# h kept in DRAM as the two parts of its split, in place of the unsplit h

## The chip, the core and the metric

The kernel runs on one core of a Trainium2 chip. The metric is the device time of one execution, in microseconds (us); lower is better. Engines: PE is TensorE (its weight loads are listed as PEld), DVE is VectorE, ACT is ScalarE, POOL is GpSimd, SP is SyncE, which issues nearly all DMAs here. A name with a q (SPq) is that engine's sequencer, which issues DMAs and waits.

## The reference

One layer of a streaming encoder on a prompt of 4096 tokens and a sample of 64, with 1024 features. Cut to what matters here:

```python
h = rms_norm(x, g_pre) * (1 + scale) + shift          # (T, 1024), scale and shift from c
q_a, k_a, v_a, z_a, a_lr, q_h, f_h, i_h, z_h = split(h @ w_in)
o_a = chunked_gla(q_a, k_a, v_a, log_alpha(a_lr))      # GLA, 4 heads
f = lb + (1 - lb) * sigmoid(f_h)
o_h = chunked_gla(silu(q_h), 1 - f, i_h, log(f))       # HGRN2, 4 heads
o = concat(rms_norm(o_a) * silu(z_a), rms_norm(o_h) * silu(z_h)) @ w_out
y = x + gate * rms_norm(o, g_post)
```

Everything is float32. All projections read the same h. The outputs are y for prompt and sample and the final states of both recurrences.

## The kernel before

**Products in parts.** A float32 product is made of three float32r products: each operand is split into a high part (a copy to float32r on ACT, L93) and a low part (the source less the high part, on DVE, L94); `split` (L87) issues both. Then high times high, high times low and low times high are added up in PSUM.

**Stages.** Tokens go in 16 groups of 256; the 64 sample tokens ride along with one group (T = 320 in place of 256), the last one in phase 1 and group 2 afterwards. Features are eight blocks of 128 (KT = 8), features on partitions. There are four stages, and each runs over all groups before the next begins, since the weights of one stage fill the weight room:

1. Phase 1 (GLA). For each group: load x, normalise, transpose and modulate it to h (`x_turn`), split h, project it (`proj_gla`), run the recurrence (`attend_group`). The unsplit h is stored to DRAM, `h_d` (and `h_s` for the sample), for the two stages that need it again.
2. HGRN. h is loaded from `h_d` (`load_hf`), split again, projected (`proj_hgrn`), and the recurrence runs. Its result goes to DRAM, `oh_d`.
3. The gate part. h is loaded and split a third time; `z_tile` projects one tile of 128 tokens (24 matmuls of 512 columns) and multiplies silu(z) into the HGRN result, which it loads from `oh_d` and stores back (L1299, L1308). The split of w_out runs beside it.
4. The output projection (`project`), which does not use h.

**The rooms of h.** Pool `h` has two tags. `hf` has four tiles of two blocks each, unsplit (float32); together one group. `hh` has five tiles, each with both parts of two blocks, so one group takes four of the five. A phase 1 group fills the four `hf` in `x_turn`; an HGRN or gate group fills them by `load_hf`. Then `split_h` makes four `hh`. The fifth `hh` lets the first split of a group start while the group before is still being projected; each further one waits until a pair of blocks of that group has been used for the last time, in the last token tile's product (`proj_tok`, L625; feature-side products are `proj_feat`, L613).

**Order.** The kernel is written against a framework that orders the instructions: it keeps a list per engine, with the order of the code as priority and its own estimate of when operands and rooms are ready, and places all semaphores. Each engine, SP with its DMAs among them, then works through its list in order, so an instruction that waits holds those behind it. `weave` runs a main generator (the projections of a group) and side generators (the recurrence of the group before as `side`, preparation of the next group as `prep`, loads of weights) in turns; the tuple (generator, n, first, last) spreads n steps between two steps of the main one.

**Lines that matter below.** The stores of h in phase 1 are L574 and L576, that of group 0 is L1663, the loads L581 and L583, `split_h` L585. `pair_up` (L595) copies the sample's columns of h on POOL. x is loaded at L475 (groups 0 and 1) and L482, and squared for its norm at L491 and L510. L1215 is the last DVE step of a recurrence result in HGRN and L1216 its store; L711 to L967 are the DVE chain of the recurrence that ends in the operands of the PE products at L1017; L1305 to L1308 end a gate tile.

Of the kernel before, what the change touches and what calls it, by code (L numbers as in the profile page):

```python
# [6 lines left out]
F32 = mybir.dt.float32  # L7
F32R = mybir.dt.float32r
# [7 lines left out]
P = 128  # L16
D = 1024
KT = D // P
GROUP = 256
# [9 lines left out]
class Kernel:  # L29
# [107 lines left out]
    def setup(self):  # L137
        nc, t, ctx = self.nc, self.t, self.ctx
        c = self.pool(ctx, "const")
        self.small = self.pool(ctx, "small", 4)  # L140
        self.wpool = self.pool(ctx, "w")

        self.wstage = self.pool(ctx, "wstage", 2, side="right")
        self.halves = []
        self.ep = self.pool(ctx, "e", side="right")
        self.h_room = ctx.enter_context(ExitStack())
        self.hp = self.pool(self.h_room, "h", side="right")
        self.x_room = ctx.enter_context(ExitStack())
        self.xp = self.pool(self.x_room, "x", side="right")
        self.pp = self.pool(ctx, "psum", 1, PSUM)  # L150
        dram = self.pool(ctx, "scratch", 1, DRAM)
        self.h_d, self.oa_d, self.oh_d = [], [], []
        for g, tl in enumerate(self.groups):
            self.h_d.append(dram.tile([P, KT, GROUP], F32, name=f"h_d{g}"))
            self.oa_d.append([dram.tile([r, 512], F32, name=f"oa_d{g}_{j}") for j, (_, _, r, _) in enumerate(tl)])
            self.oh_d.append([dram.tile([r, 512], F32, name=f"oh_d{g}_{j}") for j, (_, _, r, _) in enumerate(tl)])
        self.h_s = dram.tile([P, KT, self.dec], F32, name="h_s")
        self.gate_d = dram.tile([2, D], F32, name="gate_d")
        self.gate_p = dram.tile([8, 512], F32, name="gate_p")

        nc.scalar.preload_act_table_set("natural_log_exp_and_others")
        self.ident = c.tile([P, P], F32, name="ident")
        self.col = col = c.tile([P, 52], F32, name="col")
        self.c4 = c.tile([P, KT, 4], F32R, name="c4")
        self.md = c.tile([P, 2, KT, 2], F32, name="md")
        self.sh, self.gs = self.md[:, 0], self.md[:, 1]
        self.mask = c.tile([P, NMASK], U8, name="mask")
        self.member = c.tile([P, 12], F32, name="member")
        self.half = c.tile([P, 2], F32, name="half")
        self.balpha = col[:, 40:42]  # L170
        self.lb = c.tile([P, 4], F32, name="lb")
        self.oml = c.tile([P, 4], F32, name="oml")
        self.wal = c.tile([80, 256], F32R, name="wal")
        self.ats = [c.tile([P, 80], F32R, name=f"at{i}") for i in range(3)]

        with ExitStack() as s:
            one = self.pool(s, "setup")
            ap = self.pool(s, "ada", 3)

            rows = one.tile([52, P], F32, name="rows")  # L180
            v = lambda a: a.rearrange("(k p) -> k p", p=P)
            self.x_load(0, [0])
            nc.sync.dma_start(rows[0:8], v(t["c_prompt"][0]))
            nc.sync.dma_start(rows[8:16], v(t["c_sample"][0]))
            nc.sync.dma_start(self.ident, t["ident"])
            self.x_load(0, [1])
            few = [
                (rows[16:32], v(t["b_ada"][0, : 2 * D])),
                (rows[32:40], v(t["g_pre"][0])),
                (rows[40:42], v(t["b_alpha"][0])),  # L190
                (rows[42:50], t["hgrn_lb_logits"].rearrange("r (k p) -> (r k) p", p=P)),
                (rows[50:51], t["g_onorm_gla"]),
                (rows[51:52], t["g_onorm_hgrn"]),
            ]
            ada = self.ada_load(ap, 0, few[:4])
            w = self.first_load(0)
            for dst, src in few[4:]:
                nc.sync.dma_start(dst, src)
            with self.tc.manual_schedule():
                self.first_group(ap, ada, w, rows)  # L200
            for _ in self.vs0:
                pass
# [17 lines left out]
    def first_group(self, ap, ada, w, rows):  # L220


        nc, col = self.nc, self.col
        W = self.W1
        T = GROUP
# [98 lines left out]
        pr = self.ps("ms")  # L324
        nc.tensor.transpose(pr[:, :52], rows, self.ident[:52, :52])
        ada_sum(pa, parts.pop(0), [(1, 0), (1, 1)])
        self.hf = [self.hp.tile([P, 2, T], F32, name="hf", bufs=4) for _ in range(4)]
        nc.vector.tensor_copy(col[:, 16:], pr[:, 16:52])
        nc.vector.tensor_scalar(col[:, 24:32], col[:, 24:32], 1.0, None, ALU.add)
        raw(0, nc.scalar)  # L330
# [153 lines left out]
    def x_norm(self, g, js):  # L484

        nc = self.nc
        ss = self.small.tile([P, 2], F32, name="x_ss")
        for i, j in enumerate(js):
            xt, r = self.xs[j], self.groups[g][j][2]
            junk = self.hp.tile([P, 2, GROUP], F32, name="hf", bufs=4).rearrange("p k c -> p (k c)")  # L490
            nc.scalar.activation(  # L491
                junk.bitcast(mybir.dt.bfloat16)[:r], xt[:r], AF.Square, accum_out=ss[:r, i : i + 1]
            )
        rs = self.rstd(ss[:r, : len(js)], D, table=True)
        for i, j in enumerate(js):
            nc.vector.tensor_scalar(self.xs[j][:r], self.xs[j][:r], rs[:, i : i + 1], None, ALU.mult)
# [30 lines left out]
    def x_turn(self, g):  # L527
# [1 line left out]
        nc = self.nc  # L529
        tl = self.groups[g]  # L530
        T = self.tokens(tl)
        self.hf = hf = [self.hp.tile([P, 2, T], F32, name="hf", bufs=4) for _ in range(4)]
        for tiles, cnd in (([0, 1], 0), ([2], 1)):
            if tiles[0] >= len(tl):
                continue
# [22 lines left out]
            for i in range(4):  # L558
# [11 lines left out]
                    else:  # L570
                        nc.vector.tensor_scalar(dst, dst, sc, bi, ALU.mult, ALU.add)
                yield
        for i in range(4):
            nc.sync.dma_start(self.h_d[g][:, 2 * i : 2 * i + 2, :], hf[i][:, :, :GROUP])  # L574
            if len(tl) == 3:
                nc.sync.dma_start(self.h_s[:, 2 * i : 2 * i + 2, :], hf[i][:, :, GROUP:])  # L576

    def load_hf(self, g, tl):
        self.hf = [self.hp.tile([P, 2, self.tokens(tl)], F32, name="hf", bufs=4) for _ in range(4)]
        for i in range(4):  # L580
            self.nc.sync.dma_start(self.hf[i][:, :, :GROUP], self.h_d[g][:, 2 * i : 2 * i + 2, :])  # L581
            if len(tl) == 3:
                self.nc.sync.dma_start(self.hf[i][:, :, GROUP:], self.h_s[:, 2 * i : 2 * i + 2, :])  # L583

    def split_h(self):  # L585

        out = []
        T = self.hf[0].shape[2]
        for i in range(4):
            u = self.hp.tile([P, 2, 2, T], F32R, name="hh", bufs=5)  # L590
            self.split(u[:, 0], u[:, 1], self.hf[i])
            out.append(u)
        return lambda k: out[k // 2][:, :, k % 2]

    def pair_up(self, h, rooms):  # L595

# [1050 lines left out]
    def run(self):  # L1647
# [11 lines left out]
        with ExitStack() as rec:  # L1659
            self.open_recurrence(rec)  # L1660
            self.setup_late()
            for i in range(4):
                nc.sync.dma_start(self.h_d[0][:, 2 * i : 2 * i + 2, :], self.hf[i])  # L1663
            h = lambda k: self.h0[k // 2][:, :, k % 2]
            S, Ss = [None], [t["state_gla"]]
            side = None
# [9 lines left out]
                yield from self.x_turn(g)  # L1676

            def prep_h(g, tl):
                self.load_hf(g, tl)
                yield  # L1680

            for g in range(ng):
                prep = prep_x(g + 1) if g + 1 < ng else prep_h(0, self.groups2[0])
                sides = [(side, 12, 1, 18), (prep, 8, 0, 16) if g == 0 else (prep, 10, 3, 19)]
                if g == ng - 1:

                    sides.append((self.weights(W2["f"], C_FH, 512, "wa"), 10, 8, 18))
                    sides.append((self.weights(W2["q"], C_QH, 512, "wv"), 10, 20, 26))
                res = self.weave(self.proj_gla(g, h), sides)
                h = self.split_h()  # L1690
                side = self.attend_group(g, S, Ss, res, 2, 2, self.oa_d, t["new_gla_p"], t["new_gla_s"])
                next(side)
            S, Ss = [None], [t["state_hgrn"]]
# [2 lines left out]
            for g in range(ng):  # L1696
# [7 lines left out]
                if g == ng - 1:  # L1704
                    sides.append((self.weights(W3["z"], C_ZH, 512, "wa"), 10, 8, 18))
                res = self.weave(self.proj_hgrn(g, h), sides)
                h = self.split_h()
                side = self.attend_group(g, S, Ss, res, 4, 1, self.oh_d, t["new_hgrn_p"], t["new_hgrn_s"])
                next(side)
            now(gate)  # L1710
# [3 lines left out]
            def zrun():  # L1714
                hh = h
                for i, (g, j, tl) in enumerate(tiles):
                    if j == 0 and i > 0:
                        hh = self.split_h()
                        if len(self.groups2[g]) == 3:
                            self.pair_up(hh, [self.stage_pair(F32R)])  # L1720
                    if j == 0 and g + 1 < ng:
                        self.load_hf(g + 1, self.groups2[g + 1])
                    yield from self.z_tile(hh, tiles[i])
                    self.done += 1
                    yield
# [75 lines left out]
```

## Time and profile before

| | before |
|---|---|
| median of 3 runs | 2094.87 us (2094.38 to 2095.93) |
| profiled execution, time / span | 2090.48 us / 2088.7 us |
| PE, DVE, ACT busy | 98%, 75%, 53% of the span |
| granted PE clock, mean | 0.997 |
| DMA: bytes, mean rate | 190.15 MB, 91 GB/s |
| 128 loads `hf<-h_d`, 64 stores `h_d<-hf` | 256 KB each |
| splits of h (L93 on ACT, L94 on DVE), 188 of each | 625 ns and 697 ns, mean |

How to read it: the median is over executions without the profiler's view; the profile shows one execution, so sums made from its rows are compared with its own time. A row of an instruction group gives line, engine, operation, output<-inputs, shapes and count; then busy time and the mean ns of one; then the engine's idle time just before and what ended it. A row of a stage gives its length and each engine's busy time, the granted PE clock as a share of full speed, the DMA engines' busy share and the rate. A row of the timeline or the chain begins with its start and its length in us; [..] holds the idle time before it and what ended that. A busy PE is not PE at its peak, as matmuls overlap.

### The profile page before, as it was taken

What the parts mean: (1) busy time and instruction counts of PE and PEld (TensorE: products, weight loads), DVE (VectorE), ACT (ScalarE), POOL (GpSimd) and SP (SyncE); (2) the same over time, 40 slices, a digit from 0 to 9 for tenths busy, and PEclk for the clock granted to TensorE, in tenths of its full rate; (3) what the DMA queues carried; (4) which work ended last, traced back from release to release, by engine and by line L of the source; (5) the groups of instructions that cost most, each with busy time, mean ns of one, the idle gap of its engine ahead of it and who ended that gap; (6) DMA issues with size and microseconds to landing.
All of it is one profiled execution on the core that took longest, in us unless ns stands there. A gap on an engine that the chain in (4) does not pass through costs nothing.

```text
span 2088.7 us, 47161 instructions
## 1 busy us (share of the span) xinstructions
PE 2045.3 (98%) x17384; PEld 1804.4 (86%) x17384; DVE 1559.2 (75%) x4795; ACT 1106.4 (53%) x3238; POOL 310.2 (15%) x781
## 2 busy tenths in 40 slices
PE   8999999999999999999999999999999999999998
PEld 6888899888899888999999999999987888888886
DVE  7777777676776687778888788778787776777775
ACT  6676666676666574444445444444445544433332
POOL 0111111111111211111111111111110002232321
PEclk9999999999999999999999999999999999999999
DMA  9322222222222242011111111111145764444443
GB/s 293 94 53 75 63 63 57 52 59 71 63 62 55 67 130 70 32 36 59 47 47 47 47 34 41 52 36 32 42 131 187 234 209 152 157 147 153 150 143 100
DMA packets 236116, 190.15 MB, mean 91 GB/s; under 512 B 138220, under 2 KB 160208, under 8 KB 235884
## 3 DMA queue, kind: packets, MB, share of 16 engines
q1 hardware_dynamic: 235740, 186.86, 29.9%
q8 instruction: 137, 2.24, 0.4%
q14 instruction: 95, 0.78, 0.1%
q10 hardware_dynamic: 144, 0.26, 0.0%
HBM read 126.60 MB, written 60.45 MB: 90 GB/s over the span
## 4 chain that ended last, share of the span: by engine, by line
PE 54%; DVE 8%; ACT 2%; DMA 1%; issue 1%; SPq 0%; DVEq 0%; POOL 0%; ACTq 0%
PE ps_pj L625 15%; PE ps_pj L613 13%; PE ps_pj L1403 13%; PE ps_o L1403 2%; DVE wst L967 2%; PE ps_at L1017 2%; PE ps_ms L819 2%; PE ps_o L798 2%; PE ps_o L803 1%; PE ps_at L693 1%; DMA wst<-in_w_in_dram 1%; DVE dd L699 1%; PE ps_pj L633 1%; PE ps_at L924 1%; PE ps_tp L773 1%; PE ps_at L1394 1%
## 5 line engine op out<-in xcount | busy, mean ns | idle before, releaser
L613 PE MATMUL ps_pj<-hh,wa 128*128 128x256 f32 (+1 forms) x2976 | 394.1, 288 | 3.1 <-ACT hh L93 3.1
L613 PEld LDWEIGHTS ps_pj<-hh,wa 128*128 128x128 f32 x2976 | 375.1, 192 | 7.9 <-ACT hh L93 3.4
L625 PE MATMUL ps_pj<-wb,hh 128*128 128x512 f32 x1536 | 379.4, 397 | 0.0
L625 PEld LDWEIGHTS ps_pj<-wb,hh 128*128 128x128 f32 x1536 | 279.9, 188 | 56.7 <-issue 2.7
L613 PE MATMUL ps_pj<-hh,wv 128*128 128x256 f32 (+1 forms) x1536 | 202.0, 286 | 0.0
L613 PEld LDWEIGHTS ps_pj<-hh,wv 128*128 128x128 f32 x1536 | 189.8, 188 | 8.7 <-issue 6.9
L625 PE MATMUL ps_pj<-wv,hh 128*128 128x264 f32 x1464 | 194.6, 288 | 0.1
L625 PEld LDWEIGHTS ps_pj<-wv,hh 128*128 128x128 f32 x1464 | 182.5, 188 | 4.3 <-ACT nwt_y L76 2.2
L625 PE MATMUL ps_pj<-wa,hh 128*128 128x512 f32 x768 | 177.9, 391 | 0.0
L625 PEld LDWEIGHTS ps_pj<-wa,hh 128*128 128x128 f32 x768 | 143.3, 188 | 30.7 <-issue 0.8
L1261 ACT ACTIVATE g<-ps_pj 128x256 f32<-128x256 f32 (+1 forms) x128 | 49.5, 387 | 216.2 <-PE ps_pj L613 215.8
L94 DVE TENSOR_TENSOR hh<-hf,hh 128x512 fp32r<-128x512 f32 (+1 forms) x188 | 128.9, 697 | 38.4 <-ACT hh L93 36.4
L93 ACT CAST hh<-hf 128x512 fp32r<-128x512 f32 (+1 forms) x188 | 117.3, 625 | 66.8 <-PE ps_pj L625 48.3
L998 POOL COPY T<-T 128x16 f32<-128x16 f32 (+1 forms) x32 | 7.9, 247 | 770.3 <-DVE Qg L859 431.9
L967 DVE TENSOR_TENSOR wst<-wst,T 128x160 f32<-128x160 f32 (+4 forms) x480 | 108.4, 266 | 1.1
L991 ACT ACTIVATE A<-Ac,member 128x128 f32<-128x128 f32 x256 | 80.4, 390 | 49.2 <-DVE Ac L985 49.2
L1463 ACT ACTIVATE sq<-e 128x512 bf16<-128x512 f32 x64 | 40.4, 631 | 119.7 <-DVE e L1475 119.7
L1403 PE MATMUL ps_pj<-wc,wa 128*128 128x512 f32 x384 | 98.5, 391 | 0.0
L1466 POOL TENSOR_TENSOR e<-e,gg 128x512 f32<-128x512 f32 x32 | 41.4, 1293 | 362.6 <-ACT sq L1463 352.0
L1403 PEld LDWEIGHTS ps_pj<-wc,wa 128*128 128x128 f32 x384 | 72.0, 188 | 16.1
L1000 POOL TENSOR_TENSOR T<-T,T 128x16 f32<-128x16 f32 (+1 forms) x224 | 82.5, 368 | 17.6
L830 DVE SCALAR_TENSOR_TENSOR S<-S,T,ps_ms 128x128 f32<-128x128 f32 x186 | 55.4, 343 | 34.7 <-PE ps_ms L819 34.7
(350 smaller groups left out, 4116.3 us busy)
## 6 DMA issues: line engine op xcount, KB each, us to landing
hf<-h_d SPq DMA_DIRECT2D x128, 256.0 KB
h_d<-hf SPq DMA_DIRECT2D x64, 256.0 KB
oh_d<-e SPq DMA_DIRECT2D x64, 256.0 KB
xq<-in_x_prompt_dram SPq DMA_DIRECT2D x64, 256.0 KB
out_y_prompt_dram<-xq SPq DMA_DIRECT2D x63, 256.0 KB
xt<-in_x_prompt_dram SPq DMA_DIRECT2D x448, 32.0 KB
wst<-in_w_in_dram SPq DMA_DIRECT2D x36, 256.0 KB
e<-oh_d SPq DMA_DIRECT2D x33, 256.0 KB
```

The costliest lines, as they stand in the source:

```text
L93: self.nc.scalar.copy(hi, src)
L94: (eng or self.nc.vector).tensor_tensor(lo, src, hi.bitcast(F32), ALU.subtract)
L613: self.nc.tensor.matmul(ps[:, :T], a, b, start=i == 0, stop=i == n - 1)
L625: self.nc.tensor.matmul(ps[:r, : c1 - c0], a, b, start=kt == 0 and i == 0, stop=kt == KT - 1 and i == 2)
L798: nc.tensor.matmul(po[h], A[:, c * 4 + h, :], v, start=h < n, stop=St is None and h == 4 - n)
L819: nc.tensor.matmul(pd[s * w : (s + 1) * w, g, :], kc[:CL, g, s * w : (s + 1) * w], vs[c][:CL, h * P : (h + 1) * P], start=not apart, stop= ...
L830: nc.vector.scalar_tensor_tensor(Sn[:, g, :], St[:, g, :], T[:, c * G + g, 0:1], pd[:, g, :], ALU.mult, ALU.add)
L967: nc.vector.tensor_tensor(parts(dst), parts(src), t.unsqueeze(3).to_broadcast(shape), ALU.mult)
L991: nc.scalar.activation(Ah[:, :, 32 * b : 32 * b + 32], Ach, AF.Copy, scale=self.member[:CL, 8 + b : 9 + b])
L1000: nc.gpsimd.tensor_tensor(E8[:, :, i], E8[:, :, i - 1], T8[:, :, i], ALU.mult)
L1261: nc.scalar.activation(sg, pf[:, :T], AF.Sigmoid)
L1403: nc.tensor.matmul(bank, u[:, a, kt, :], W[name][kt][:, b], start=kt + i == 0, stop=kt + i == 5)
```

## The change

DRAM holds the two parts of every block of h, in place of h. A phase 1 group stores them after its split (`keep_h`, eight stores from the `hh` tiles, in place of four from `hf`). HGRN and the gate part no longer split: they load the parts block by block (`load_h`), blocks 0, 1, 4 and 5 into two `hh` tiles and blocks 2 and 3 into two rooms of the tag `hf`, which a group of theirs now leaves half empty. These six are asked for where `load_hf` was. Blocks 6 and 7 take a third `hh` tile and are asked for where the split was (`loaded`), since a group then holds three of the five `hh` tiles and the next one can have two. The stores of group 0 move from before the weave of phase 1 into it, as a side generator of steps 10 to 16.

```diff
-            self.h_d.append(dram.tile([P, KT, GROUP], F32, name=f"h_d{g}"))
+            self.h_d.append(dram.tile([P, KT, 2, GROUP], F32, name=f"h_d{g}"))
...
     def x_turn(self, g):
...
-        for i in range(4):
-            nc.sync.dma_start(self.h_d[g][:, 2 * i : 2 * i + 2, :], hf[i][:, :, :GROUP])
-            if len(tl) == 3:
-                nc.sync.dma_start(self.h_s[:, 2 * i : 2 * i + 2, :], hf[i][:, :, GROUP:])
-
-    def load_hf(self, g, tl):
...
-    def split_h(self):
+    def split_h(self, g):
         out = []
...
             self.split(u[:, 0], u[:, 1], self.hf[i])
             out.append(u)
+        for _ in self.keep_h(g, out):
+            pass
         return lambda k: out[k // 2][:, :, k % 2]
+
+    def keep_h(self, g, tiles):
+        for i, u in enumerate(tiles):
+            u = u.bitcast(F32)
+            for k in range(2):
+                self.nc.sync.dma_start(self.h_d[g][:, 2 * i + k], u[:, :, k, :GROUP])
+                if u.shape[3] > GROUP:
+                    self.nc.sync.dma_start(self.h_s[:, 2 * i + k], u[:, :, k, GROUP:])
+            yield
+
+    def load_h(self, g, tl, last=False):
+        T = self.tokens(tl)
+        if not last:
+            self.hnext = {}
+        for k in range(6, 8) if last else range(6):
+            if k in (2, 3):
+                u = self.hp.tile([P, 2, T], F32R, name="h1", tag="hf", bufs=4)
+            else:
+                if k % 2 == 0:
+                    two = self.hp.tile([P, 2, 2, T], F32R, name="hh", bufs=5)
+                u = two[:, k % 2]
+            raw = u.bitcast(F32)
+            self.nc.sync.dma_start(raw[:, :, :GROUP], self.h_d[g][:, k])
+            if T > GROUP:
+                self.nc.sync.dma_start(raw[:, :, GROUP:], self.h_s[:, k])
+            self.hnext[k] = u
+
+    def loaded(self, g, tl):
+        self.load_h(g, tl, last=True)
+        h = self.hnext
+        return lambda k: h[k]
...
-            for i in range(4):
-                nc.sync.dma_start(self.h_d[0][:, 2 * i : 2 * i + 2, :], self.hf[i])
...
+                if g == 0:
+                    sides.append((self.keep_h(0, self.h0), 4, 10, 16))
...  # phase 1, after proj_gla(g, h)
-                h = self.split_h()
+                h = self.split_h(g + 1) if g + 1 < ng else self.loaded(0, self.groups2[0])
...  # HGRN, after proj_hgrn(g, h)
-                h = self.split_h()
+                h = self.loaded((g + 1) % ng, self.groups2[(g + 1) % ng])
...  # gate part, at the first tile of a group
-                        hh = self.split_h()
+                        hh = self.loaded(g, self.groups2[g])
...
-                        self.load_hf(g + 1, self.groups2[g + 1])
+                        self.load_h(g + 1, self.groups2[g + 1])
```

More of the change, by code (lines that the diff above doesn't have):

```diff
@@ L153, in setup @@
         for g, tl in enumerate(self.groups):
-            self.h_d.append(dram.tile([P, KT, GROUP], F32, name=f"h_d{g}"))
+            self.h_d.append(dram.tile([P, KT, 2, GROUP], F32, name=f"h_d{g}"))
             self.oa_d.append([dram.tile([r, 512], F32, name=f"oa_d{g}_{j}") for j, (_, _, r, _) in enumerate(tl)])
             self.oh_d.append([dram.tile([r, 512], F32, name=f"oh_d{g}_{j}") for j, (_, _, r, _) in enumerate(tl)])
-        self.h_s = dram.tile([P, KT, self.dec], F32, name="h_s")
+        self.h_s = dram.tile([P, KT, 2, self.dec], F32, name="h_s")
         self.gate_d = dram.tile([2, D], F32, name="gate_d")
@@ L326, in first_group @@
         ada_sum(pa, parts.pop(0), [(1, 0), (1, 1)])
-        self.hf = [self.hp.tile([P, 2, T], F32, name="hf", bufs=4) for _ in range(4)]
+        self.hf = [self.hp.tile([P, 2, T], F32, name="hf", tag="hf", bufs=4) for _ in range(4)]
         nc.vector.tensor_copy(col[:, 16:], pr[:, 16:52])
@@ L489, in x_norm @@
             xt, r = self.xs[j], self.groups[g][j][2]
-            junk = self.hp.tile([P, 2, GROUP], F32, name="hf", bufs=4).rearrange("p k c -> p (k c)")
+            junk = self.hp.tile([P, 2, GROUP], F32, name="hf", tag="hf", bufs=4).rearrange("p k c -> p (k c)")
             nc.scalar.activation(
@@ L531, in x_turn @@
         T = self.tokens(tl)
-        self.hf = hf = [self.hp.tile([P, 2, T], F32, name="hf", bufs=4) for _ in range(4)]
+        self.hf = hf = [self.hp.tile([P, 2, T], F32, name="hf", tag="hf", bufs=4) for _ in range(4)]
         for tiles, cnd in (([0, 1], 0), ([2], 1)):
@@ L572, in x_turn @@
                 yield
-        for i in range(4):
-            nc.sync.dma_start(self.h_d[g][:, 2 * i : 2 * i + 2, :], hf[i][:, :, :GROUP])
-            if len(tl) == 3:
-                nc.sync.dma_start(self.h_s[:, 2 * i : 2 * i + 2, :], hf[i][:, :, GROUP:])
-    def load_hf(self, g, tl):
-        self.hf = [self.hp.tile([P, 2, self.tokens(tl)], F32, name="hf", bufs=4) for _ in range(4)]
-        for i in range(4):
-            self.nc.sync.dma_start(self.hf[i][:, :, :GROUP], self.h_d[g][:, 2 * i : 2 * i + 2, :])
-            if len(tl) == 3:
-                self.nc.sync.dma_start(self.hf[i][:, :, GROUP:], self.h_s[:, 2 * i : 2 * i + 2, :])
-    def split_h(self):
+    def split_h(self, g):
         out = []
@@ L1661, in run @@
             self.setup_late()
-            for i in range(4):
-                nc.sync.dma_start(self.h_d[0][:, 2 * i : 2 * i + 2, :], self.hf[i])
             h = lambda k: self.h0[k // 2][:, :, k % 2]
@@ L1678, in prep_h @@
             def prep_h(g, tl):
-                self.load_hf(g, tl)
+                self.load_h(g, tl)
                 yield
```

## The prediction

> **What bounds the kernel now.** I read the page's busy shares first, then the table by stage, then the chain of waits, then who PE waited for. The stages: start-up to 75 us, GLA (phase 1) to about 775, HGRN to 1540, the gate part to 1736, then the output projection. Columns of a stage row: length, PE, PEld, DVE, ACT and POOL busy, granted clock, DMA share, GB/s.
>
> ```profile
> span 2088.7 us, 47161 instructions
> PE 2045.3 (98%) x17384; PEld 1804.4 (86%) x17384; DVE 1559.2 (75%) x4795; ACT 1106.4 (53%) x3238; POOL 310.2 (15%) x781
> 775.00:1540.00 765.00, 755.51 (x7457) 697.46 (x7456) 617.76 (x2089) 364.93 (x1031) 96.94 (x343) 1.00 0.15 45
> 1540.00:1736.00 196.00, 195.04 (x1029) 159.98 (x1028) 138.01 (x283) 92.28 (x172) 8.48 (x25) 1.00 0.62 202
> 1591.00:1722.00 131.00, 131.00 (x579) 108.48 (x578) 91.22 (x146) 65.57 (x109) 0.00 (x0) 1.00 0.67 219
> 1438.60:1484.70 46.10, 46.00 (x462) 43.15 (x461) 36.48 (x122) 21.43 (x62) 5.31 (x19) 1.00 0.12 36
> 1433.19 2.77 PE ps_pj L625 x12
> 1438.63 8.18 PE ps_pj L625 x36
> 1446.81 4.32 PE ps_pj L613 x36
> 1591.18 136.04 PE ps_pj L625 x600
> ```
>
> PE is the limit in both stages that the change relieves: one HGRN group (1438.6 to 1484.7) has PE busy 46.0 of 46.1 us, and in the gate part the chain is 600 matmuls in a row. HGRN leaves 765.00 - 755.51 = 9.5 us without PE, the gate part 1.0. That is all that the removal of ACT and DVE work can give there, unless matmuls run faster. I see no sign of that: 8.18/36 = 227 ns beside 36 GB/s of DMA, 136.04/600 = 227 ns beside 219 GB/s.
>
> **The change, part by part.** Removed splits: of 47 calls of split_h, 32 go (16 for HGRN, 16 for the gate part), each four ACT copies (L93) and four DVE subtractions (L94).
>
> ```profile
> L94 DVE TENSOR_TENSOR hh<-hf,hh 128x512 fp32r<-128x512 f32 (+1 forms) x188 | 128.9, 697 | 38.4 <-ACT hh L93 36.4 <-DMA hf<-h_d 1.1
> L93 ACT CAST hh<-hf 128x512 fp32r<-128x512 f32 (+1 forms) x188 | 117.3, 625 | 66.8 <-PE ps_pj L625 48.3 <-DMA hf<-h_s 8.6 <-ACT hh L93 2.4
> PE ps_at L1017 <- DVE wst L967: 8.1, 17, 1.6
> PE ps_pj L613 <- ACT hh L93: 3.1, 1, 3.1
> 1490.71 1.29 DVE L94 TENSOR_TENSOR hh<-hf,hh 128x512 fp32r<-128x512 f32 x2
> 1494.02 0.69 DVE L94 TENSOR_TENSOR hh<-hf,hh 128x512 fp32r<-128x512 f32 x1 [1.15 <-ACT hh L93]
> 1497.64 0.69 DVE L711 TENSOR_TENSOR A<-Xg,K 128x512 f32<-128x512 f32 x1 [2.92 <-PE ps_at L693]
> ```
>
> That is 128 x 0.625 = 80 us of ACT and 128 x 0.697 = 89 us of DVE. On the path it is almost nothing. PE waited on a split once, 3.1 us near 710 us, and that split belongs to phase 1 and stays. What PE does wait for from 775 us on is DVE's L967 (8.1 us in 17 waits), yet that chain begins at L711, before which DVE stood idle for 2.92 us waiting on PE, after the last split had ended at 1494.7. So the splits do not make L967 late. HGRN: between -2.0 (9.5 idle less the 7.5 or so of L967) and 0; I take -0.5. Gate part: between -1.0 and 0; I take -0.5.
>
> DMA: the DRAM copy doubles, a transfer stays 256 KB and their number doubles.
>
> ```profile
> hf<-h_d SPq DMA_DIRECT2D x128, 256.0 KB
> h_d<-hf SPq DMA_DIRECT2D x64, 256.0 KB
> 20.00:25.00 5.00, 3.92 (x28) 3.26 (x27) 4.20 (x13) 2.69 (x6) 0.00 (x0) 1.00 1.16 318
> 50.00:55.00 5.00, 3.74 (x28) 2.92 (x27) 2.59 (x6) 2.69 (x6) 0.00 (x0) 1.00 1.02 386
> ```
>
> Loads go from 128 to 256 and stores from 64 to 128: 192 x 0.262 MB = 50 MB more. In HGRN (15% DMA share) this is covered. The gate part is the place to worry. A group is 48 matmuls x 0.227 = 10.9 us there and gets four more loads, 1.05 MB, or 96 GB/s. From 219 GB/s at a share of 0.67 that makes 315 GB/s at 0.96. Full queues moved 318 and 386 GB/s in the start-up rows, so I take it as just fitting, at 0; the upper end is in the rivals.
>
> The last two blocks. Blocks 6 and 7 get the room of the running group's blocks 0 and 1, free after 6 of the 24 matmuls of its last token tile: 18 x 0.227 = 4.1 us before that group ends. The next group needs block 6 after 18 matmuls: in HGRN 18 x 0.120 = 2.2 us (4.32/36), in the gate part 4.1 us. The lead is 6.3 and 8.2 us. What a load takes:
>
> ```profile
> 1510.09 2.66 DMA wst<-in_w_in_dram
> 1560.46 5.08 DMA hf<-h_s
> 1483.74 7.41 SPq L1216 DMA_DIRECT2D oh_d<-e  x2
> 1490.11 0.69 DVE L1215 TENSOR_TENSOR e<-e,nwt_y 128x512 f32<-128x512 f32 x1
> 1491.43 3.63 SPq L581 DMA_DIRECT2D hf<-h_d  x4
> 1640.22 0.60 ACT L1305 ACTIVATE e<-ps_pj 128x512 f32<-128x512 f32 x1 [3.29 <-PE ps_pj L625]
> 1642.30 0.32 SPq L1308 DMA_DIRECT2D oh_d<-e  x1
> ```
>
> Some 0.35 us to issue and 2.7 to 5.1 us to land (the 5.1 stood behind other loads) is 3.0 to 5.4 us, inside both leads. But SP works in its written order, and the order decides whether these loads stand ahead of the store of the group's result, whose wait would hold them. In HGRN the store waits for L1215, which ends at 1490.8; loads behind it land from about 1493.9 to 1496.6, against a need at 1492.85 + 2.2 = 1495.0: 0 to 1.6 us a group. In the gate part the store goes out at 1642.30, 2.1 us after the tile's end (L1305 starts at 1640.22); loads behind it land 5.1 to 7.9 us into a group that needs them at 4.1: 1.0 to 3.8 us. The rooms come free 4.1 us before the tile ends and the store 2.1 after, so in an order made by readiness the loads go first. I take 0.
>
> Queued behind each such wait on SP are the six early loads, and they have a whole group. POOL's only reader of h, pair_up, waits for a load in place of a split. GLA: SP issues four more DMAs a group, 4 x 0.35 = 1.4 us, and the stores now wait for the split, with the next group's x loads behind them.
>
> ```profile
> L510 ACT ACTIVATE sqx<-xt 128x256 bf16<-128x256 f32 x114 | 47.3, 415 | 2.2
> 35.61 0.57 SPq L1663 DMA_DIRECT2D h_d<-hf  x1
> 40.98 1.40 SPq L1663 DMA_DIRECT2D h_d<-hf  x1
> 46.75 0.91 SPq L475 DMA_DIRECT2D xt<-in_x_prompt_dram  x2
> 52.94 1.06 ACT L491 ACTIVATE hf<-xt 128x1024 bf16<-128x1024 f32 x1 [1.20 <-DMA xt<-in_x_prompt_dram]
> ```
>
> ACT's first reader of those loads idled 2.2 us in the whole run, so x is early; if that cover is gone, up to 14 x 1.4 = 20 us. I take 0. Start-up: DMA is saturated, and x of group 1 lands late enough to hold ACT for 1.20 us. Ahead of it stood two 256 KB stores. If the new stores move behind it, those 1.2 us go; if they are issued as early as before, there are four, and 0.52 MB more at 318 GB/s is 1.65 us later. Between -1.2 and +1.65, I take +0.2.
>
> Sum against the profiled execution's own 2090.48 us (span 2088.7 and 1.8 around it): -0.5 - 0.5 + 0 + 0 + 0.2 = -0.8, so 2089.7. The three timed runs have a median of 2094.87, 4.4 above the profiled one; carried over, 2094.1, say **2094**. About 0.2% (4.2 us) is what a measurement of this kernel can tell from no change.
>
> [...] The PE wait near 710 us shows what a longer stall costs.
>
> ```profile
> 709.00:711.00 2.00, 0.43 (x1) 0.43 (x2) 2.00 (x7) 2.00 (x5) 0.00 (x0) 0.71 0.47 99
> 711.00:713.00 2.00, 2.00 (x9) 1.96 (x9) 2.00 (x4) 1.40 (x3) 1.45 (x1) 0.50 0.32 80
> 715.00:717.00 2.00, 2.00 (x10) 2.00 (x9) 2.00 (x9) 0.31 (x1) 2.00 (x5) 0.58 0.69 253
> ```
>
> After the 3.1 us wait the granted clock was 0.50 until past 715 us: about 5.5 us at half speed, 2.7 us more lost. [...]
>
> [...]
>
> **The rivals.** Faster: the freed ACT and DVE time lets the schedule close HGRN's gaps and the 710 us spot. Its price is at most 9.5 + 3.1 + 2.7 = 15 us; half of it gives 2094.9 - 7.5, about 2087. For it speaks DVE's 81% in HGRN; against it that DVE waits on PE before the chain that PE waits for. Blocks 6 and 7 behind the store on SP (slower): 15 groups x 1.0 to 3.8 in the gate part = 15 to 57 us, so 2110 to 2152; it decides once the loads are issued more than 4.1 - 2.7 = 1.4 us after the group's start. Against it speaks the order by readiness; for it, that SP's 3.63 us of four loads began only after L1215's store. The gate part bound by DMA (slower): if the queues hold 287 GB/s, about 10% under the start-up row, 315/287 over 131 us is +12.8, 2107; with less shortage, from 2099. For it speaks the share of 0.96. GLA and start-up (slower): x loads or stores in the way, +1.65 at start-up and a quarter of the 20 us, about 2101. That the change does not do what it says, with the early loads not early, I rule out: the rooms of six blocks are free when the previous group ends, some 11 or 46 us ahead.
>
> **How the numbers follow.** No change, 2090 to 2099: 0.45. Faster: 0.20. Behind the store: 0.11. DMA-bound: 0.14. GLA and start-up: 0.10. Slower is 0.35 in all. The range reaches into the faster case to 2086 and over the DMA-bound and GLA cases to 2109; outside stay the store rival and the far half of the faster one.
>
> **What would show it.** Right: L93 and L94 on hh drop from 188 to 60, ACT near 1026 and DVE near 1470 us busy, PE busy as before, a gate part of still about 10.9 us a group with DMA share over 0.9, no wait of PE on a DMA into hh. Wrong: rows of PE or PEld at L613 or L625 waiting on a DMA from h_d, a granted clock under 1.0 in the gate part, or HGRN groups clearly under 46.0 us.

## The result and the profile after

The changed kernel takes 2107.26 us (median of four runs, 2105.1 to 2114.2) against 2094.72 for the kernel before on the same chip: ratio 1.007, 95% interval 1.0054 to 1.0085, so 12.5 us slower. The forecast was no change. The profiled execution took 2108.12 us (span 2106.3). Its difference of 17.6 us to the profiled execution before holds some 5 us of chance: that one lay 4.4 us below its median, this one 0.9 above.

The page of the changed kernel, and its two groups of splits of h:

```profile
span 2106.3 us, 46927 instructions
PE 2050.6 (97%) x17384; PEld 1808.3 (86%) x17384; DVE 1482.0 (70%) x4667; ACT 1033.8 (49%) x3110; POOL 310.1 (15%) x781
DMA packets 283921, 241.25 MB, mean 115 GB/s; under 512 B 144556, under 2 KB 200336, under 8 KB 283692
L94 DVE TENSOR_TENSOR hh<-hf,hh 128x512 fp32r<-128x512 f32 (+1 forms) x60 | 41.5, 696 | 10.5 <-ACT hh L93 10.0
L93 ACT CAST hh<-hf 128x512 fp32r<-128x512 f32 (+1 forms) x60 | 37.2, 623 | 1.2 <-DVE hf L555 1.2
```

The edit did what it says: 60 splits of each kind in place of 188, DVE 77 us and ACT 73 us less busy, 51 MB more on the queues. To see where the time went I cut both spans at the same four instructions: the first product L1157 (L1182 after; lines behind `keep_h` move down by 25) of the first and of the last GLA group, an HGRN tile's first L625 (L650), and the last L625 of the gate part. Stage rows, columns as in the prediction: before, then after.

```profile
0.00:80.12 80.12, 68.18 (x436) 52.22 (x437) 59.18 (x127) 52.82 (x100) 6.32 (x15) 1.00 0.79 233
80.12:759.71 679.59, 667.73 (x6754) 599.95 (x6752) 481.16 (x1756) 447.70 (x1567) 92.43 (x321) 0.99 0.27 65
759.71:1478.99 719.28, 710.36 (x7014) 655.85 (x7013) 580.32 (x1954) 345.67 (x968) 92.18 (x324) 1.00 0.15 46
1478.99:1734.46 255.47, 253.95 (x1556) 213.40 (x1555) 188.14 (x449) 122.41 (x258) 14.69 (x44) 1.00 0.52 170
```

```profile
0.00:82.88 82.88, 69.85 (x436) 53.74 (x437) 59.19 (x127) 52.82 (x100) 6.32 (x15) 0.98 0.81 238
82.88:770.24 687.36, 669.15 (x6754) 601.47 (x6752) 482.19 (x1755) 447.89 (x1566) 94.26 (x321) 1.00 0.35 88
770.24:1490.02 719.78, 710.28 (x7015) 655.82 (x7013) 542.93 (x1894) 311.22 (x909) 89.73 (x324) 1.00 0.21 68
1490.02:1752.00 261.98, 256.23 (x1556) 214.19 (x1554) 147.38 (x382) 84.05 (x191) 15.17 (x44) 0.99 0.71 235
```

Start-up +2.8, GLA +7.8, HGRN +0.5, the rest of HGRN with the gate part +6.5; the output projection is as before. So HGRN, where 64 of the 128 removed splits stood, neither gains nor loses, and the loss sits in GLA, which lost no split, and in the gate part.

**GLA.** Before, the groups from the fourth to the fourteenth all took 44.5 to 44.6 us; after, the eighth to the thirteenth take 45.1, 45.2 and 44.8 in a cycle of three. One group of each:

```profile
433.65:478.24 44.59, 44.16 (x451) 39.59 (x450) 31.54 (x116) 29.45 (x104) 5.69 (x21) 1.00 0.25 61
```

```profile
440.10:485.30 45.20, 44.21 (x452) 39.50 (x450) 31.22 (x114) 29.44 (x104) 5.69 (x21) 1.00 0.34 84
```

PE has the same work and, in this group, 1.0 us of idle time in place of 0.4. What it waits for in six groups (total, times, longest), before and after:

```profile
PE ps_ms L1129 <- DVE at L1124: 0.9, 6, 0.2
```

```profile
PE ps_ms L1154 <- DVE at L1149: 3.3, 6, 0.8
```

DVE's timeline ahead of that wait in the group above shows why; below it is the same place before, one group after the one shown:

```profile
470.16 0.55 DVE L919 TENSOR_TENSOR K<-K,T 128x384 f32<-128x384 f32 x1
471.73 1.10 DVE L562 STREAM_TRANSPOSE hf<-xt 128x256 f32<-128x256 f32 x3 [1.03 <-ACT xt L523]
...
473.25 0.17 DVE L1149 TENSOR_TENSOR at<-ps_pj,at 128x16 fp32r<-128x16 f32 x1
```

```profile
507.86 0.77 DVE L562 STREAM_TRANSPOSE hf<-xt 128x256 f32<-128x256 f32 x2 [2.24 <-ACT xt L523]
...
509.06 0.55 DVE L894 TENSOR_TENSOR K<-K,T 128x384 f32<-128x384 f32 x1
...
510.05 0.18 DVE L1124 TENSOR_TENSOR at<-ps_pj,at 128x16 fp32r<-128x16 f32 x1
```

Three transposes L562, which prepare the next group's h, stand in DVE's list between L919 and the chain L1140 to L1149 that PE needs. DVE waits 1.03 us for ACT to hand them their operand, does them, and only then takes up the chain. Before, two of them stood ahead of the last product of that line (L894 there). The other two groups of the cycle have one and two transposes in the place of before, and PE waits 0.5 and 0.4 us. In all three the norm of the next group moved too: its DVE step L514 stands behind the group's first L1149 (467.14 and 463.30 us here), where before it stood ahead (499.15 and 501.77 us). So the order of DVE's list has changed.

Late x is not the reason. ACT waited for a load of x in one of these six groups, for 0.8 us, and in none before; that group took 45.21 us, and its like in the cycle without such a wait 45.20.

Such groups are not all of GLA's 7.8 us. The sixth to the fourteenth hold 3.8 of them; the third to the fifth took 4.9 us more than before, the last one 1.6 more, and the first two 2.5 less. The waits in those were not followed row by row; the experiments show whether the same cause holds for them.

**The gate part.** From 1602 us on, nine of the twelve groups take 10.88 us as before; two are 0.2 and 0.3 us longer, and one takes 16.8 us. SP and PE around that one:

```profile
1696.19 0.50 SPq L1324 DMA_DIRECT2D e<-oh_d  x1
1696.79 1.27 SPq L1368 DMA_DIRECT2D wst<-in_w_out_dram  x2
1702.74 0.33 SPq L1333 DMA_DIRECT2D oh_d<-e  x1
...
1703.64 1.84 SPq L610 DMA_DIRECT2D hh<-h_d  x4
...
1706.68 0.96 PE L650 MATMUL ps_pj<-wa,hh 128*128 128x512 f32 x3 [1.78 <-DMA hh<-h_d]
1709.54 3.74 PE L650 MATMUL ps_pj<-wa,hh 128*128 128x512 f32 x9 [1.90 <-DMA hh<-h_d]
```

The first two of the four loads at 1703.64 are blocks 6 and 7 of the group that began at 1700.66. They stand on SP behind the store L1333, which waits until 1702.74. It belongs to the first of the two tiles of the group before, which ended at 1695.22. Its product needs the `oh_d` load issued at 1696.19 and starts at 1702.03; that load shares full queues with two w_out loads of 512 KB (316 GB/s at a share of 0.96 from 1696 to 1700 us). SP waited for such loads in front of 11 stores between 1540 and 1750 us (total, times, longest), and only behind this one did PE wait. PE waits 3.7 us, and the granted clock falls as well:

```profile
SPq L1333 <- DMA e<-oh_d: 27.5, 11, 4.6
1710.14:1713.55 3.41, 3.41 (x10) 2.67 (x9) 0.69 (x1) 1.62 (x3) 0.00 (x0) 0.50 1.03 394
```

### The profile page after: what moved, and what is told of

It reads as the page before. It is cut to its first block, busy times and chain, and to the rows that moved or that the text cites. A ratio compares the mean times of both kernels' runs of the same rounds, so it can differ in the third digit from the quotient of the medians.

```text
span 2106.3 us, 46927 instructions
## 1 busy us (share of the span) xinstructions
PE 2050.6 (97%) x17384; PEld 1808.3 (86%) x17384; DVE 1482.0 (70%) x4667; ACT 1033.8 (49%) x3110; POOL 310.1 (15%) x781
## 4 chain that ended last, share of the span: by engine, by line
PE 52%; DVE 7%; DMA 3%; ACT 1%; issue 1%; SPq 0%; POOL 0%; DVEq 0%; POOLq 0%; ACTq 0%
PE ps_pj L638 14%; PE ps_pj L650 13%; PE ps_pj L1428 13%; PE ps_o L1428 2%; DMA e<-oh_d 2%; DVE wst L992 2%; PE ps_at L1042 2%; PE ps_ms L844 2%; PE ps_o L823 2%; PE ps_o L828 1%; PE ps_at L718 1%; PE ps_pj L658 1%; PE ps_tp L798 1%; PE ps_at L949 1%; PE ps_at L1419 1%
## 5 line engine op out<-in xcount | busy, mean ns | idle before, releaser
L638 PE MATMUL ps_pj<-hh,wa 128*128 128x256 f32 (+1 forms) x2592 | 353.4, 289 | 3.5 <-ACT hh L93 2.8
L638 PEld LDWEIGHTS ps_pj<-hh,wa 128*128 128x128 f32 x2592 | 330.9, 192 | 8.9 <-ACT hh L93 3.0
L650 PE MATMUL ps_pj<-wb,hh 128*128 128x512 f32 x1344 | 337.1, 398 | 0.0
L650 PEld LDWEIGHTS ps_pj<-wb,hh 128*128 128x128 f32 x1344 | 245.6, 189 | 50.1 <-issue 2.7
L650 PE MATMUL ps_pj<-wv,hh 128*128 128x264 f32 x1464 | 193.6, 287 | 0.1
L650 PEld LDWEIGHTS ps_pj<-wv,hh 128*128 128x128 f32 x1464 | 182.1, 188 | 4.3 <-ACT e L1138 2.6
L638 PE MATMUL ps_pj<-hh,wv 128*128 128x256 f32 (+1 forms) x1152 | 163.2, 287 | 0.0
L638 PEld LDWEIGHTS ps_pj<-hh,wv 128*128 128x128 f32 x1152 | 147.3, 188 | 8.0 <-issue 6.7
L650 PE MATMUL ps_pj<-wa,hh 128*128 128x512 f32 x576 | 140.9, 395 | 3.7 <-DMA hh<-h_d 3.7
L650 PEld LDWEIGHTS ps_pj<-wa,hh 128*128 128x128 f32 x576 | 108.1, 189 | 28.2 <-DMA hh<-h_d 5.5
L992 DVE TENSOR_TENSOR wst<-wst,T 128x160 f32<-128x160 f32 (+3 forms) x480 | 108.1, 266 | 1.2
L1206 ACT COPY v<-ps_pj 128x512 f32<-128x512 f32 x64 | 37.4, 585 | 103.4 <-PE ps_pj L650 103.0
L961 ACT COPY A<-ps_at 32x128 f32<-32x128 f32 (+4 forms) x288 | 75.8, 291 | 7.8 <-PE ps_at L949 5.3
```

Of the source, the lines that this page charges most:

```text
L638: self.nc.tensor.matmul(ps[:, :T], a, b, start=i == 0, stop=i == n - 1)
L650: self.nc.tensor.matmul(ps[:r, : c1 - c0], a, b, start=kt == 0 and i == 0, stop=kt == KT - 1 and i == 2)
L961: nc.scalar.copy(A.rearrange("p (g two s) c -> p s two g c", two=2, s=NS)[m * b : m * b + m, s, odd, :, P - w :], pas[s][m * r : m * r + m ...
L992: nc.vector.tensor_tensor(parts(dst), parts(src), t.unsqueeze(3).to_broadcast(shape), ALU.mult)
```

## The experiments

Each median is compared with the kernel before, timed beside it. Its median was 2094.74 us for four runs (h's stores on POOL, twice the stores, no HGRN operand, the gate part's store on POOL), 2093.47 for four (whole tiles, the moved pair, both stores on POOL with and without the change) and 2094.13 for four (another order, fewer bytes, the two with group 0's stores on SP).

### Stores of h on POOL's queue

```diff
-                self.nc.sync.dma_start(self.h_d[g][:, 2 * i + k], u[:, :, k, :GROUP])
+                self.nc.gpsimd.dma_start(self.h_d[g][:, 2 * i + k], u[:, :, k, :GROUP])
```

> The changed kernel with one edit: keep_h's stores of the two parts (L591, L593) go out on POOL's queue in place of SP's. Bytes and rooms are as in the changed kernel. Theory A (SP's order: the eight stores wait for the split and stand among the 32 x loads of a group, which moves the x loads, and with them the order of DVE's work in front of PE's L1154): a GLA group goes from 45.1 back to 44.6 us, PE's waits on L1149 from 3.3 to about 1 us in six groups, start-up loses most of its +2.8, the whole -7 to -10 us, 2097 to 2100. Rival B (the bytes: twice the stores in flight): nothing moves, GLA groups stay at 45.1, 2107. Either way the gate part keeps its wait on blocks 6 and 7.

2099.0 us, ratio 1.0023 (1.0012 to 1.0034): 8.3 less than the changed kernel. A group at the same place, DVE's list there, and PE's only wait in six groups:

```profile
441.65:486.18 44.53, 44.13 (x453) 39.59 (x452) 31.79 (x117) 29.68 (x105) 11.52 (x30) 1.00 0.33 84
464.55 0.77 DVE L562 STREAM_TRANSPOSE hf<-xt 128x256 f32<-128x256 f32 x2 [2.60 <-ACT xt L523]
...
465.75 0.55 DVE L919 TENSOR_TENSOR K<-K,T 128x384 f32<-128x384 f32 x1
PE ps_o L823 <- ACT A L961: 1.2, 6, 0.2
```

The queues carry the same 84 GB/s, and two transposes stand ahead of L919's last products again, in every group. The bytes in flight are not what GLA pays for; what stands in SP's list is. That holds for the uneven groups too: all of GLA took 676.7 us, 10.6 less than in the changed kernel, and the third to the fifth group 44.5 to 44.6 each. ACT waited for loads of x here as well, 3.2 us in three of the first groups, and the third and the fourth were as short as before all the same. The expected fall of start-up did not come (first product at 84.02 us). The gate part kept its stall, with 5.2 us of PE's waits.

### Twice the stores, from the unsplit h

```diff
             nc.sync.dma_start(self.h_d[g][:, 2 * i : 2 * i + 2, :], hf[i][:, :, :GROUP])
+            nc.sync.dma_start(self.h_e[g][:, 2 * i : 2 * i + 2, :], hf[i][:, :, :GROUP])
```

> The kernel before, with each of groups 1 to 15 storing its unsplit h twice, the second time into a DRAM copy that nobody reads: the count and the bytes of stores of the changed kernel in GLA, without the wait for the split and with nothing changed in start-up, HGRN or the gate part. If number and bytes of the stores on SP are what GLA pays for: about +0.5 us a group, 2094.7 + 7 = 2102. If it is that the stores wait for the split: no change, 2095.

2102.11 us, ratio 1.0045 (1.0031 to 1.006). GLA groups of 45.1 and 45.7 us in turn, and the same wait:

```profile
PE ps_ms L1132 <- DVE at L1127: 5.4, 6, 1.3
```

So the wait for the split is not needed for the loss: the added stores on SP do it alone.

### As many stores as before, of twice the size

```diff
-            for k in range(2):
-                self.nc.sync.dma_start(self.h_d[g][:, 2 * i + k], u[:, :, k, :GROUP])
+            self.nc.sync.dma_start(self.h_d[g][:, i], u[:, :, :, :GROUP])
```

> The changed kernel with another layout of h_d (pair of blocks, part, block), so that a phase 1 group stores each hh tile by one DMA of 512 KB on SP: four stores a group in place of eight, as many as before the change, in the same places of SP's order, behind the split. The loads stay eight of 256 KB. If the number of DMAs on SP is what GLA pays for: groups of 44.6 us, about -7, 2100. If it is their bytes or their place behind the split: groups stay at 45.1, 2107. The gate part's stall stays either way.

2109.14 us, ratio 1.0074 (1.006 to 1.0087). The groups take 45.20, 44.78 and 45.13 us, within 0.03 us those of the changed kernel. The count of DMAs is not needed for the loss either. Together: the three kernels that pay share one thing, twice the bytes of stores in SP's list, and with the same bytes on POOL's queue nothing is paid. So these bytes in SP's list move DVE's order, although at run time the bytes as such cost nothing; no run changes the bytes alone. Such an order comes from the framework's estimates of when a queue has done its work; that it is its estimate for SP that moves is an inference from these three runs.

### Another order with the same stores

```diff
-                sides = [(side, 12, 1, 18), (prep, 8, 0, 16) if g == 0 else (prep, 10, 3, 19)]
+                sides = [(side, 12, 1, 18), (prep, 8, 0, 16) if g == 0 else (prep, 10, 0, 16)]
```

> The changed kernel with the preparation of the next group in phase 1 (x_turn and its norm) spread from step 0 to 16 of a group's projections in place of 3 to 19. Stores, queues and bytes as in the changed kernel. In DVE's order of the changed kernel one, two or three copies L562 stand in turn ahead of the chain that ends in L1149, a cycle of three groups of 45.2, 44.8 and 45.1 us; with this edit the order from the eighth group on is the same in every group, two copies ahead, as before the change. Theory A (GLA pays through DVE's order, not through SP's time or the bytes): groups 8 to 13 take 44.5 to 44.6 us, 6 x 0.5 = 3 us less, near 2104; the first groups stay uneven. Rival (SP's queue or the stores themselves): groups stay at 45.1, 2107.

2113.68 us, ratio 1.0099 (1.0084 to 1.0115). Both expectations failed: the groups are alike from the seventh on, but at 46.15 us.

```profile
500.00:546.15 46.15, 44.06 (x452) 39.87 (x451) 31.25 (x117) 29.68 (x104) 5.66 (x21) 1.00 0.33 81
PE ps_at L949 <- DVE wst L919: 1.0, 1, 1.0
PE ps_o L823 <- ACT A L961: 0.6, 1, 0.6
PE ps_ms L1154 <- DVE at L1149: 0.5, 1, 0.5
```

With the same stores on the same queue the order alone makes a group 1.0 us longer, by three waits that add up to the 2.1 us without PE. I had counted the transposes in front of L1149 and had not looked at those further up, in front of L919. That the order decides is borne out; how an order is to be read was too simple.

### The gate part without its HGRN operand

```diff
-        oh = self.etile()[:r]
-        nc.sync.dma_start(oh, o_d)
...
-        nc.vector.tensor_tensor(oh, oh, e, ALU.mult)
-        nc.sync.dma_start(o_d, oh)
```

> The changed kernel without the gate part's load of the HGRN result, its last product and its store (L1324, L1332, L1333): the gate of HGRN is left out of the output. That takes 1.05 MB a group off the DMA queues, what the parts of h added, and takes the store off SP, in front of blocks 6 and 7. Theory A (late blocks 6 and 7, by the queue's load or by the store): no wait of PE on hh<-h_d, 10.9 us in every group of the gate part, -6 us, 2101. Rival (the loads of the parts are late by themselves, or matmuls run slower beside them): 2107.

2099.53 us, ratio 1.0023 (1.0014 to 1.0032): no wait of PE on a load, 10.9 us in every group. It says that the stall belongs to this traffic or to this store, not which.

### The gate part's store on POOL's queue

```diff
-        nc.sync.dma_start(o_d, oh)
+        nc.gpsimd.dma_start(o_d, oh)
```

> The changed kernel with the gate part's store of the HGRN result (L1333) on POOL's queue in place of SP's: all bytes stay, but nothing on SP waits for the gated tile any more. Theory A (the loads of blocks 6 and 7 stand on SP behind a store whose operand is late): PE's waits on hh<-h_d in the gate part go, 10.9 us a group, -6 us, 2101. Rival B (the DMA queues are full, 311 GB/s at a share of 0.92): the loads land as late as now, the waits stay at 3.7 us and the clock falls with them, 2107.

2100.69 us, ratio 1.0031 (1.0019 to 1.0043): 6.6 less than the changed kernel, and no wait. The same 96 us of the gate part in the changed kernel, then here:

```profile
1640.00:1736.00 96.00, 92.31 (x396) 74.87 (x395) 42.32 (x66) 28.28 (x44) 0.00 (x0) 0.98 0.92 311
```

```profile
1640.00:1736.00 96.00, 96.00 (x425) 79.51 (x424) 45.17 (x69) 28.41 (x45) 9.76 (x18) 1.00 0.91 316
```

PE is busy without a gap beside 316 GB/s. The queues carry all that the change asks of them; without the store in SP's list there is no stall.

### The pair of w_out loads at another group

```diff
-            self.weave(until(len(tiles) - 3), [(self.load_wout(room), 44, 0, 62)])
+            self.weave(until(len(tiles) - 3), [(self.load_wout(room), 44, 0, 66)])
```

> The changed kernel with the 44 steps of the load and split of w_out spread over 66 steps of the gate part in place of 62. In the changed kernel SP's order has one place where two w_out loads of 512 KB stand back to back ahead of a gated tile's store and of blocks 6 and 7, at the thirteenth group, the one with the stall; here that place is at the eighth group. Theory A (this place in SP's order makes the stall): the stall of 2.2 + 2.3 us moves to the eighth group and the thirteenth runs in 10.9 us; the time stays at 2107 or a little under. Rival (a backlog of the DMA queues that builds up over the gate part): the stall stays near 1704 us, whatever the order.

2104.32 us, ratio 1.0051 (1.0039 to 1.0063). The larger part of the stall moved with the pair, to a group that begins at 1641.34 and asks for its blocks 6 and 7 1.2 us after its beginning:

```profile
1635.40 1.25 SPq L1368 DMA_DIRECT2D wst<-in_w_out_dram  x2
1641.63 0.33 SPq L1333 DMA_DIRECT2D oh_d<-e  x1
...
1642.53 1.81 SPq L610 DMA_DIRECT2D hh<-h_d  x4
PE ps_pj L650 <- DMA hh<-h_d: 2.7, 4, 1.3
1644.00:1648.00 4.00, 2.55 (x10) 1.45 (x9) 0.69 (x1) 0.60 (x1) 0.00 (x0) 1.00 0.98 310
```

Near the old place two groups are 0.6 and 1.1 us longer. This stall costs 2.3 us, not 5.9: PE waited 1.7 us in place of 3.7, and the clock stayed at 1.00. So a place in SP's order decides where it comes, not a backlog that builds up over the stage.

### Fewer bytes in about the same order

```diff
-        nc.sync.dma_start(oh, o_d)
+        nc.sync.dma_start(oh[:, :256], o_d[:, :256])
...
-        nc.sync.dma_start(o_d, oh)
+        nc.sync.dma_start(o_d[:, :256], oh[:, :256])
```

> The changed kernel whose gate part loads, multiplies and stores only the first 256 of the 512 columns of the HGRN result (the second half of the gate of HGRN is left out of the output): 0.52 MB a group less on the queues, 15%, while in SP's order blocks 6 and 7 of the thirteenth group still stand behind the pair of w_out loads and the gated tile's store. If the order alone makes the stall: 4 to 6 us stay lost there. If it takes the full queues as well, which hold up the load that the store waits for: the stall falls under 2 us, 2107 - 4 = 2103 or less.

2099.33 us, ratio 1.0032 (1.0021 to 1.0044), and no wait at all. Blocks 6 and 7 still stand behind the pair and the store, but the store now goes out at 1696.05 and the loads at 1696.47, 2.0 us ahead of their group, which begins at 1698.47; in the changed kernel they went out 3.0 us after it had begun.

```profile
1696.05 0.33 SPq L1333 DMA_DIRECT2D oh_d<-e  x1
1696.47 1.82 SPq L610 DMA_DIRECT2D hh<-h_d  x4
1640.00:1736.00 96.00, 96.00 (x425) 79.53 (x424) 39.82 (x69) 27.23 (x44) 0.00 (x0) 1.00 0.80 263
```

The load of the store's operand was hardly faster: it was issued at 1690.44 and its product started 5.2 us later, against 5.8 us in the changed kernel. But it was issued 8.0 us ahead of the group, in place of 4.5, as SP had got further in its list. The stall takes both: the order, and queues so full that SP falls behind in its list (311 GB/s at a share of 0.92 over the 96 us of the changed kernel, 263 at 0.80 here). Either one removed, it is gone.

### Both stores on POOL, with and without the change

The edits above together, on the changed kernel; the same two moves on the kernel before; and each of the two with group 0's stores left on SP (`nc.sync` for g == 0).

> The changed kernel with both edits of the two runs before: keep_h's stores and the gate part's store on POOL's queue. If GLA's part (-8.3, measured) and the gate part's (-6.6, measured) are separate waits on SP: they add up, 2107.3 - 14.9 = 2092.4, GLA groups of 44.5 us and gate groups of 10.9. If the one stall only moves (POOL now carries two kinds of stores): 2099 or more.

> The kernel before with the same stores on POOL's queue: those of the unsplit h in phase 1 and that of the gate part; nothing else of the change. It tells what the relief of SP is worth by itself. Theory A (the removed splits are worth nothing on the path, and what the changed kernel with both stores on POOL gains over 2094.7 comes from SP): the same time as that kernel, 2092 +- 1. Rival (the change has a gain of its own that SP's waits had covered): this one stays at 2095 and the other is below it by 2 us or more.

> The kernel before with the stores of h of groups 1 to 15 and the gate part's store on POOL's queue; group 0's stores stay on SP. Same as the earlier run with all stores on POOL but for start-up, where the first GLA product came at 89.26 us against 80.12 before. Theory: that was the whole loss of it, and this one is back at 80 to 81 us there, total 2098.6 - 8.5 = 2090 to 2094, with GLA groups of 44.5. If POOL's queue cost something elsewhere: 2096 or more. Beside the changed kernel with the same queues it tells what the change itself is worth: nothing by the forecast's working, so both within 2 us.

> The changed kernel with keep_h's stores of groups 1 to 15 and the gate part's store on POOL's queue, group 0's stores on SP as in the changed kernel. Against both stores on POOL (2093.2; first GLA product at 82.23 us): if group 0's stores on POOL cost start-up something, 80 to 83 us there and 2091 to 2093; if not, the same 2093.

| | median, us | ratio to before | first GLA product, us |
|---|---|---|---|
| changed, both stores on POOL | 2093.2 | 0.9992 (0.9984 to 1.0001) | 82.23 |
| changed, the same but group 0's stores on SP | 2092.36 | 0.9995 (0.9986 to 1.0004) | 80.22 |
| before, both stores on POOL | 2098.64 | 1.0023 (1.0014 to 1.0032) | 89.26 |
| before, the same but group 0's stores on SP | 2090.64 | 0.9985 (0.9976 to 0.9994) | 79.80 |

The two losses add up: 14.1 us come back of the changed kernel's 2107.26, where the parts alone gave 8.3 and 6.6. The control with all of its stores on POOL missed its 2092 through start-up, 9.1 us longer than before. There PE waited 4.6 us in one place and 3.5 in another, where the kernel before waits 2.6 and at most 0.7, and the granted clock was 0.95 on the mean of the first 75 us in place of 1.00. Why those waits grew was not followed:

```profile
PE ps_ms L1129 <- DVE at L1124: 4.6, 1, 4.6
PE ps_ms L257 <- ACT e L249: 3.5, 1, 3.5
```

With group 0 back on SP this control is at 2090.64 us, faster than both kernels, with GLA groups as short as with the change:

```profile
389.48:433.97 44.49, 44.10 (x452) 39.59 (x451) 31.77 (x116) 29.63 (x106) 7.85 (x25) 1.00 0.25 61
```

The like-for-like pair is 2092.36 with the change and 2090.64 without. Their intervals against the kernel before overlap, but in 102 of the 121 pairs of their executions the one without the change is the shorter: freed of SP's waits, the change gains nothing and rather loses some 2 us. Of the 4.3 us between their profiled executions 3.3 lie in the last GLA group (61.24 against 57.92 us), and from 711 to 775 us the granted clock was 0.93 on the mean with the change and 0.99 without. The control with all of its stores on POOL had 0.92 there, so that the change causes it is not shown.

## Why the prediction was wrong

**The removed splits (right).** HGRN was put at -0.5 and is at +0.5 by the stage rows, 0 by the group: 46.09 us in place of 46.10, with DVE 2.6 us less busy. PE's wait on the recurrence's operands hardly cared (8.1 us before, 6.9 after), as the prediction argued from L711:

```profile
1443.93:1490.02 46.09, 45.99 (x464) 43.12 (x462) 33.87 (x118) 18.98 (x57) 5.35 (x19) 1.00 0.18 59
PE ps_at L1042 <- DVE wst L992: 6.9, 15, 1.3
```

**GLA, taken as 0 (wrong, 8.3 us).** This step failed. The prediction asked whether four more DMAs on SP would make x late, found ACT's first reader of x idle for only 2.2 us in the whole run, and closed the term. Afterwards ACT did wait for x in GLA, four times and 4.3 us in all, but in the group that has a like one to compare this cost nothing. The step looked for a wait at run time in an order taken as given; but all engines' lists are made anew from the framework's estimates, and with the new stores next-group work on DVE moved in front of what PE needs. The runs show the link from SP's list to DVE's order; that it passes through the estimates is inferred. The rival for GLA had the place and the sign, with 5 of the 7.8 us, by the wrong mechanism: x loads in the way.

**Blocks 6 and 7 in the gate part, taken as 0 (wrong in one group, 6.6 us).** This step failed too: "in an order made by readiness the loads go first". The prediction set the loads against the store of a group's last tile. They stand beside that of its first tile, which goes out near the time at which their rooms come free. Of the twelve groups that begin between 1613 and 1740 us, five have both loads ahead of it, four only block 6, and three neither. One of these three begins at 1634.80:

```profile
1633.77 0.32 SPq L1333 DMA_DIRECT2D oh_d<-e  x1
1634.18 1.82 SPq L610 DMA_DIRECT2D hh<-h_d  x4
```

Here the store was early enough, and PE did not wait. In the group at 1700.66 the second rival's mechanism came true, loads behind a store that is late. The rival's limit of 1.4 us into the group was a little high: 3.0 us was far too late, 1.2 cost 2.3 us (with the w_out pair moved), 2.0 ahead was in time. Its price was wrong, 15 groups at 1.0 to 3.8 us where one group paid 5.9: waits of 3.7, and 2.2 more, of which 3.4 us at a clock of 0.50 make 1.7. The prediction had not asked what else stands in that list: the pair of w_out loads.

**DMA as "just fitting" (right).** It said 315 GB/s at 0.96; the store on POOL's queue shows 316 at 0.91 with PE busy throughout. The third rival, a gate part bound by DMA, met the measured 2107 by luck and is refuted as a bound; full queues were needed for the stall only as what made the store late. The store on POOL's queue left the rate about as it was (311 and 316 GB/s); what it saved was the wait of the loads behind it.

**A wait of PE and the clock after it.** The prediction read a clock of 0.50 for about 5.5 us after a wait of 3.1 us. Here two waits of 1.78 and 1.90 us with 0.96 us of matmuls between were followed by a clock of 0.50 for 3.4 us, so the fall came without a wait as long as that; 0.38 and 1.28 us, with the pair moved, left it at 1.00. No threshold follows from these runs: in start-up PE waited 2.56 us in the kernel before, up to 72.40 us, and 2.57 us in the changed kernel, up to 73.67; the clock stayed at 1.00 in the first and was 0.50 from 76 to 78 us in the second.

**Start-up, taken as +0.2 (in its bounds at a clock of 1.00).** In the changed kernel's profile the first GLA product comes at 82.88 us, with a mean granted clock of 0.98 up to it; in that of the kernel before at 80.12 us, with 1.00. The run with the pair moved has the changed kernel's start-up, and there the clock was 1.00 and the product came at 80.03 us:

```profile
0.00:80.03 80.03, 67.82 (x436) 51.89 (x437) 59.15 (x127) 52.75 (x100) 6.32 (x15) 1.00 0.83 246
```

So with the clock at 1.00 the new start-up costs nothing that this profile shows. Whether it makes the fall of the clock more likely is open.

**"What would show it".** The counts and busy times came about as forecast (60 splits, ACT 1034, DVE 1482). Of the signs of failure, PE waiting on loads from `h_d` and a clock under 1.0 in the gate part both came. None of the signs looked at GLA, which was the larger half.

## What to carry to other kernels

Where a framework makes the order, adding DMAs to one queue can also change another engine's list, as it changed DVE's here (GLA groups of 45.1 us in place of 44.6): compare the lists and the time of one group in stages that the change hardly touches before looking for late data. A store whose operand comes late does not belong on the queue that issues the loads that PE needs next (one group of 16.8 us in place of 10.9 here); on another engine's queue it moved a like amount here (316 and 311 GB/s) and held no load. That queue is no free place either: with group 0's stores on POOL the control's first GLA product came 9.1 us later. And the work taken off engines that do not bound a stage was worth nothing in HGRN (groups of 46.09 us in place of 46.10), so the traffic added to pay for it had to be free, which it was (316 GB/s with PE busy throughout), and its place in the lists too, which it was not.

## What the runs showed of the hardware

One core's queues carried 316 GB/s of mixed 256 KB and 512 KB loads and stores at a share of 0.91 without holding PE (the gate part's store on POOL). Issuing a store of 256 KB took POOL 0.73 us (median, parts of h in GLA) where SP took 0.46; for the unsplit h it was 0.54 and 0.33. The clock was 0.50 for 3.4 us after two waits of 1.78 and 1.90 us (the changed kernel), and stayed at 1.00 after one of 2.56 us (the kernel before). And with the same start-up the first GLA product came at 82.88 us at a mean granted clock of 0.98 and, with the pair of w_out loads moved, at 80.03 us at 1.00.
